# Operand placement, the first MLP quarter's order and the last output tiles of a two-layer hybrid decoder trunk

## The chip, the cores and the metric

The kernel runs on one core of one Trainium2 chip. The metric is the device time of one execution in microseconds; the median of several runs is compared. A profile of one execution gives, for each engine, every instruction with its start and duration. TensorE multiplies matrices (PE; its weight loads are shown as PEld), VectorE (DVE) and ScalarE (ACT) work elementwise, GpSimd (POOL) does so too and issues some DMAs, and SyncE (SP) issues the other DMAs.

## The reference

One sequence of 512 tokens, width 1024, passes two layers. Each has a token mixer, an MLP with a squared ReLU and a gated per-layer embedding; a norm ends the trunk.

```python
for i in range(DEPTH):                                   # DEPTH = 2
    hn = rmsnorm(h, norm_mix_g[i])
    h = h + (even_mixer(hn, ...) if i % 2 == 0 else odd_mixer(hn, ...))   # attention
    hn = rmsnorm(h, norm_mlp_g[i])
    u = jnp.square(jax.nn.relu(hn @ w_mlp_up[i]))        # 1024 -> 4096
    h = h + u @ w_mlp_down[i]                            # 4096 -> 1024
    gate = jax.nn.sigmoid(rmsnorm(h, norm_ple_g[i]) @ w_ple_gate[i])
    h = h + (p[i] @ w_ple_proj[i]) * gate
return rmsnorm(h, final_norm_g)
```

## The kernel before

All products run in a two-part format: an operand x is split into a high part hi (a rounded copy, made by ScalarE) and a low part lo = x - hi (a subtraction, by VectorE or GpSimd), and `mm3` (lines 145 to 149) issues three matmuls for one product: hi by hi, lo by hi, hi by lo. Activations are held transposed, features in the partitions and 512 tokens along the free dimension.

**The MLP of a layer** (`mlp`) goes in four quarters (`ch`) of the hidden width. A quarter has four up units (`up`, `c` = 0 to 3), each making 256 hidden columns, and then one down part (`down`). An up unit is either plain (two accumulators, 48 matmuls of 512 columns) or, for the pairs listed in `SEVEN`, computed as seven half-size products (Strassen's scheme, `up_products`, 84 matmuls of 256 columns). The seven-product units need sums and differences of the input's token halves: `combine_inputs(m)` makes them for two of the eight input tiles: two scaled copies by ScalarE (line 765), four differences on VectorE (753 to 756), a high part by ScalarE (769) and two low parts by GpSimd (771). All units of the first quarter (`ch` = 0) are plain, and the combinations are first used in the second quarter.

Each up unit ends in a chain over the single-buffered tile `u`: relu and scaling (844), square (845), differences (846 to 850), high part `uh` (852), low part `ul` (853), four buffers each.

**The down part** is also a seven-product scheme over halves of tokens and of output columns, and over two blocks `b` of hidden rows (`b` = 0 from units 0 and 1, `b` = 1 from units 2 and 3): `product(key, b, ...)`, 14 of them with 12 matmuls each. Their weights are loaded by `fetch` into two `raw` tiles and three `q` tiles (`quarter()`, three buffers, also used by the up units and by `combine_inputs(0)` and `(1)`); `put` adds one weight block onto another (912), `take` splits a block into high and low (779, 780); `collect` copies an accumulator out by ScalarE (929) and adds it into a DRAM array with a DMA. In the first quarter, before the change, combinations 2 and 3 are made within the down part, in the `u` buffer, and the products run 4, 1, 5 of block 0, then 1, 4 of block 1, 6 (0), 5 (1), 6 (1), 2 (0), 7 (0), 7 (1), 2 (1), 3 (0), 3 (1).

**The order of the work.** A planner puts each engine's instructions in an order at build time: an instruction is placed when, by a cost model, its inputs are ready and its engine is free, and among the ready ones the one written first goes first. `order(later, earlier)` adds an edge that the planner must respect. On the chip each engine runs its list strictly in that order, and so does SP its list of DMAs.

**Memory layout.** Pools lie one behind the other in the order of their opening, tiles within a pool in the order of first use of their tags, each rounded up to 32 bytes per partition: four built-in constants, cpool (ident, ones_r, eps_n, eps_s, h, gcols, gsub, neglam, lsum), wpool (raw, wh, wl), apool (hi, lo), spool (e, rs0, rcol, the small col tiles, rs1), and then, alternately, the mixer's pool and the MLP's pool `fpool`.

**The end of layer 1** (`ple_final`) makes the gated embedding and the final norm by tiles `t` of 128 tokens, columns 0 to 511 (`c` = 0) and then 512 to 1023 (`c` = 1). For `c` = 1 each tile has a sigmoid (1176), a product and a sum on VectorE (1177, 1178), a sum of squares (1184), for tiles 0 and 1 an inverse root by eleven operations on single columns (1193, 1194, 275 to 281), a scaling of the left half by ScalarE (1121) and of the right half by VectorE (1122), and output DMAs. The sigmoid's own accumulation runs 24 matmuls ahead of it; the last tile is cut in two pieces of 256 columns. Tiles 2 and 3 get their inverse roots together, by ScalarE's Ln and Exp and one Newton step, after the last piece; tile 3 is then sent as one DMA and tile 2 as two.

Of the kernel before, what the change touches and what calls it, by code (L numbers as in the profile page):

```python
# [12 lines left out]
F32 = mybir.dt.float32  # L13
# [6 lines left out]
P = 128  # L20
# [13 lines left out]
LOAD = (3, 1)  # L34
WARM = 10
# [29 lines left out]
def trunk(  # L65
# [29 lines left out]
    def col(name="c"):  # L95
        return spool.tile([P, 6], F32, tag="col", name=nm(name), bufs=10)
# [98 lines left out]

    ident = const([P, P], "ident")
# [5 lines left out]
    eps_n = const([P, 1], "eps_n")  # L202
    nc.vector.memset(eps_n, NORM_EPS)
    eps_s = const([P, 1], "eps_s")
# [81 lines left out]
    def tok_cols(rstd):  # L286
        rp = ps("tp")
        for t in range(QT):
            nc.tensor.transpose(rp[:, t * P:(t + 1) * P], rstd[:, t * P:(t + 1) * P], ident)
        rc = spool.tile([P, QT], F32, tag="rcol", name=nm("rcol"), bufs=2)  # L290
        nc.vector.tensor_scalar(rc, rp.rearrange("p (t c) -> p t c", c=P)[:, :, 0], -0.5, None, op0=ALU.mult)
        return rc
# [4 lines left out]
    gcols = const([P, 49], "gcols")  # L297
    gsub = const([P, 1], "gsub")
    neglam = const([P, 1], "neglam")
# [35 lines left out]
    def prepare():  # L335
# [19 lines left out]
        lsum = const([P, 2], "lsum")  # L355
# [36 lines left out]
    def mixer(layer, norm, nxt):  # L392
        st = ExitStack()
        mpool = st.enter_context(tc.tile_pool(name=f"mpool{layer}", bufs=2))
        mix[:] = [mpool]
# [12 lines left out]
        keep = [] if layer else [mpool.tile([P, S + 8], F32, tag=f"keep{x}", name=nm("keep"), bufs=1) for x in range(2)]  # L408
# [335 lines left out]
    def mlp(layer, fpool, norm, nxt):  # L744
# [13 lines left out]
        def combine_inputs(m):  # L758
            if m < 2:
                u = quarter().rearrange("p a c -> p (a c)").rearrange("p (a c) -> p a c", a=4)  # L760
            else:
                u = fpool.tile([P, 7, HW], F32, tag="u", name=nm("u"), bufs=1)[:, 0:4]
            for j in range(2):
                k = 2 * m + j
                nc.scalar.activation(
                    u[:, 2 * j:2 * j + 2].rearrange("p a c -> p (a c)"), h[k], AF.Copy, scale=gcol(1, layer, k))
            differences(u)
            hi, lo = (fpool.tile([P, 4, HW], F32R, tag=f"{t}{m}", name=nm(t), bufs=1) for t in ("th", "tl"))
            nc.scalar.activation(hi, u, AF.Copy)
            for x in (slice(0, 2), slice(2, 4)):  # L770
                nc.gpsimd.tensor_tensor(lo[:, x], u[:, x], hi[:, x].bitcast(F32), op=ALU.subtract)
            (h0, l0), (h1, l1) = ahl[2 * m], ahl[2 * m + 1]
            left, right = slice(0, HW), slice(HW, S)
            combos.append({T1: (hi[:, 0], lo[:, 0]), T3: (hi[:, 1], lo[:, 1]), T4: (hi[:, 2], lo[:, 2]), T2: (hi[:, 3], lo[:, 3]),
                           B11: (h0[:, left], l0[:, left]), B21: (h1[:, left], l1[:, left]), B22: (h1[:, right], l1[:, right])})
# [114 lines left out]
        def down(ch):  # L890
# [55 lines left out]
            take(0, A22, "5")  # L946
            take(1, A11, "1")
# [4 lines left out]
            put(0, A22, A11)  # L952
# [4 lines left out]
            take(1, A22, "5")  # L957
            product("4", 1, T4, "4")
# [3 lines left out]
            take(0, A12, "2")  # L962
            take(1, A22, "6")
            if first:
                combine_inputs(2)
# [16 lines left out]
            product("2", 0, B21, "1", "mm")  # L982
# [4 lines left out]
            if first:  # L987
                combine_inputs(3)
# [56 lines left out]
        for ch in range(NCH):  # L1045
            for c in range(4):
                up(ch, c)
                if (ch, c) in ((0, 1), (0, 2)):
                    combine_inputs(c - 1)
# [66 lines left out]
    def ple_final(layer, fpool, norm, pj, rest, quarter, hk, gb, ssqn):  # L1116
        ahl = norm.hl
        ssq = [fpool.tile([P, 3], F32, tag=f"ssq{t}", name=nm("ssq"), bufs=1) for t in range(QT)]

        def finish(t, r, left, right):  # L1120
            nc.scalar.activation(hk[t][:, 0:512], hk[t][:, 0:512], AF.Copy, scale=r)
# [18 lines left out]
        for c in range(2):  # L1140
# [27 lines left out]
            for t in range(QT):  # L1168
                last = c == 1 and t == QT - 1
                for i, (c0, n) in enumerate(parts[t]):  # L1170
# [5 lines left out]
                    sg = nc.scalar.activation(gt, accs[t][i][:, 0:n], AF.Sigmoid, scale=rc[:, t:t + 1])  # L1176
                    nc.vector.tensor_tensor(gt, gt, pj[4 * c + t][:, c0:c0 + n], op=ALU.mult)
# [10 lines left out]
                if t <= QT - 2:  # L1188
                    m, r, w = (fpool.tile([P, 2], F32, tag="fin", name=nm("fin"), bufs=6) for _ in range(3))
                x = slice(t // (QT - 1), t // (QT - 1) + 1)  # L1190
                sq = ssq[t]
                small = nc.gpsimd if last else nc.vector
                small.tensor_tensor(m[:, x], sq[:, 0:1], sq[:, 1:2], op=ALU.add)
                small.tensor_scalar(m[:, x], m[:, x], 1.0 / D, NORM_EPS, op0=ALU.mult, op1=ALU.add)
                if t < QT - 2:
                    rsqrt_cols(r[:, x], m[:, x], w[:, x])
                    finish(t, r[:, x], nc.sync, nc.sync)
                elif last:
                    tables = use_tables([sg.ins])
                    ln = nc.scalar.activation(r[:, 0:1], m[:, 0:1], AF.Ln)  # L1200
                    order(ln.ins, tables)
                    nc.scalar.activation(r[:, 1:2], sq[:, 2:3], AF.Ln, scale=1.0 / D, bias=m[:, 1:2])
                    nc.scalar.activation(r, r, AF.Exp, scale=-0.5)
                    nc.vector.scalar_tensor_tensor(m[:, 1:2], sq[:, 2:3], 1.0 / D, m[:, 1:2], op0=ALU.mult, op1=ALU.add)
                    newton(r, m, w)
        finish(QT - 1, r[:, 1:2], nc.sync, None)
        finish(QT - 2, r[:, 0:1], nc.scalar, nc.sync)

# [104 lines left out]
```

## Time and profile before

| | us |
|---|---|
| median of 3 runs | 1284.85 (1284.69 to 1286.22) |
| profiled execution, its own time | 1284.56 |
| span of its instructions | 1282.7 |
| TensorE busy in the span | 1258.7 |
| VectorE busy | 1074.7 |
| ScalarE busy | 786.9 |
| GpSimd busy | 273.2 |

The profile has a page and answers to queries. A row of a group of instructions reads: line, engine, operation, output<-inputs, shape, count | busy us, mean ns of one | idle time before them and what ended it. A row of a timeline reads: start us, duration, engine, line, operation, and in brackets the idle time of the engine before it and what released it. A row of a stretch reads: from:to, length, then busy us and count for each engine, the share of the clock that TensorE was granted, the DMA engines' busy share and GB/s. Matmuls are pipelined, so the duration of one (some 0.4 us) is longer than the distance from one start to the next; distances are a stretch's length over the number of starts.

### The profile page before, as it was taken

What the parts mean: (1) busy time and instruction counts of PE and PEld (TensorE: products, weight loads), DVE (VectorE), ACT (ScalarE), POOL (GpSimd) and SP (SyncE); (2) the same over time, 40 slices, a digit from 0 to 9 for tenths busy, and PEclk for the clock granted to TensorE, in tenths of its full rate; (3) what the DMA queues carried; (4) which work ended last, traced back from release to release, by engine and by line L of the source; (5) the groups of instructions that cost most, each with busy time, mean ns of one, the idle gap of its engine ahead of it and who ended that gap; (6) DMA issues with size and microseconds to landing.
All of it is one profiled execution on the core that took longest, in us unless ns stands there. A gap on an engine that the chain in (4) does not pass through costs nothing.

```text
span 1282.7 us, 18283 instructions
## 1 busy us (share of the span) xinstructions
PE 1258.7 (98%) x6802; PEld 1078.1 (84%) x6802; DVE 1074.7 (84%) x1685; ACT 786.9 (61%) x1291; POOL 273.2 (21%) x236
## 2 busy tenths in 40 slices
PE   9999999999899999999999999999999999999996
PEld 7988887888698898988889888788878889888885
DVE  7788898798888898889777777887898988988866
ACT  6667868575565565555556666765555656555563
POOL 3443433410210200200034333221112020020101
PEclk9999999999999999999999999999999999999998
DMA  6322414241372843944233212122426356286421
GB/s 223 135 84 82 142 64 140 81 147 52 118 199 55 200 136 99 249 143 134 99 132 102 87 67 88 61 91 82 132 79 168 115 119 193 60 226 223 129 69 66
DMA packets 44026, 156.25 MB, mean 122 GB/s; under 512 B 5089, under 2 KB 5825, under 8 KB 35361
## 3 DMA queue, kind: packets, MB, share of 16 engines
q1 hardware_dynamic: 35440, 139.62, 31.8%
q0 software_dynamic: 8064, 14.68, 7.6%
q8 instruction: 53, 0.87, 0.3%
q10 hardware_dynamic: 432, 0.79, 0.2%
q14 instruction: 37, 0.30, 0.1%
HBM read 129.82 MB, written 23.15 MB: 119 GB/s over the span
## 4 chain that ended last, share of the span: by engine, by line
PE 81%; DVE 10%; ACT 4%; issue 2%; POOL 1%; DMA 1%; SPq 0%; DVEq 0%; ACTq 0%
PE mm L145 11%; PE mm L148 11%; PE mm L149 11%; PE tp L145 5%; PE tp L149 5%; PE tp L148 5%; PE sc L145 5%; PE sc L149 5%; PE sc L148 5%; PE pv L145 4%; PE pv L149 4%; PE pv L148 4%; PE pv L585 2%; PE tp L564 2%; PE sc L541 1%
## 5 line engine op out<-in xcount | busy, mean ns | idle before, releaser
L130 POOL TENSOR_TENSOR wl<-raw,wh 128x512 fp32r<-128x512 f32 (+1 forms) x132 | 180.3, 1389 | 284.4 <-ACT wh L126 267.2
L145 PE MATMUL mm<-hi,wh 128*128 128x512 f32 (+1 forms) x456 | 175.6, 385 | 0.5 <-DVE tmp L502 0.4
L149 PE MATMUL mm<-hi,wl 128*128 128x512 f32 (+1 forms) x456 | 173.5, 381 | 0.0
L148 PE MATMUL mm<-lo,wh 128*128 128x512 f32 (+1 forms) x456 | 173.3, 380 | 0.0
L126 ACT ACTIVATE wh<-raw 128x1024 fp32r<-128x1024 f32 (+1 forms) x116 | 118.8, 1028 | 55.4 <-PE mm L148 22.4
L780 DVE TENSOR_TENSOR wl<-q,wh 128x1024 fp32r<-128x1024 f32 x88 | 107.5, 1222 | 30.2 <-ACT wh L779 30.1
L779 ACT ACTIVATE wh<-q 128x1024 fp32r<-128x1024 f32 x88 | 93.0, 1057 | 62.6 <-DVE q L912 19.9
L149 PEld LDWEIGHTS mm<-hi,wl 128*128 128x128 f32 x456 | 85.8, 188 | 16.9
L145 PEld LDWEIGHTS mm<-hi,wh 128*128 128x128 f32 x456 | 85.8, 188 | 15.4 <-DVE tmp L502 0.8
L148 PEld LDWEIGHTS mm<-lo,wh 128*128 128x128 f32 x456 | 85.9, 188 | 13.2
L780 DVE TENSOR_TENSOR wl<-raw,wh 128x1024 fp32r<-128x1024 f32 x72 | 88.9, 1235 | 3.9 <-ACT wh L779 3.9
L853 DVE TENSOR_TENSOR ul<-u,uh 128x1792 fp32r<-128x1792 f32 x32 | 64.8, 2024 | 32.4 <-ACT uh L852 32.4
L558 ACT ACTIVATE e<-e,cols 128x128 f32<-128x128 f32 (+3 forms) x96 | 53.8, 561 | 60.3 <-DVE cols L555 59.9
L779 ACT ACTIVATE wh<-raw 128x1024 fp32r<-128x1024 f32 x72 | 76.0, 1056 | 22.6 <-PE mm L149 6.6
L852 ACT ACTIVATE uh<-u 128x1792 fp32r<-128x1792 f32 x32 | 54.5, 1704 | 38.4 <-DVE u L850 38.4
L932 POOL DMA_DIRECT2D part<-e x24 | 25.9, 1138 | 228.0 <-ACT e L929 228.0
L132 DVE TENSOR_TENSOR wl<-raw,wh 128x1024 fp32r<-128x1024 f32 x50 | 62.8, 1262 | 9.8 <-ACT wh L126 9.8
L573 DVE TENSOR_TENSOR ptl<-tp,pth 128x128 fp32r<-128x128 f32 (+1 forms) x112 | 54.0, 485 | 6.4 <-ACT pth L572 6.1
L572 ACT ACTIVATE pth<-tp 128x128 fp32r<-128x128 f32 (+1 forms) x112 | 47.7, 429 | 18.9 <-PE tp L564 18.4
L145 PE MATMUL sc<-wh,uh 128*128 128x512 f32 x128 | 51.8, 405 | 4.5 <-ACT e L929 4.5
L145 PE MATMUL tp<-wh,uh 128*128 128x512 f32 x128 | 51.8, 405 | 2.8 <-DVE e L998 2.8
L149 PE MATMUL mm<-wh,lo 128*128 128x256 f32 x192 | 54.3, 283 | 0.0
(402 smaller groups left out, 3903.0 us busy)
## 6 DMA issues: line engine op xcount, KB each, us to landing
raw<-in_w_up_dram SPq DMA_DIRECT2D x32, 1024.0 KB, 6.4
raw<-in_w_in_dram SPq DMA_DIRECT2D x23, 1024.0 KB, 4.9
q<-in_w_down_dram SPq DMA_DIRECT2D x32, 512.0 KB, 4.1
raw<-in_w_down_dram SPq DMA_DIRECT2D x32, 512.0 KB, 4.6
part<-e POOLq DMA_DIRECT2D x48, 256.0 KB, 7.2
raw<-in_w_gate_dram SPq DMA_DIRECT2D x8, 1024.0 KB, 5.6
bias<-urow SPq DMA_DIRECT2D x24, 256.0 KB, 3.3
raw<-in_w_outa_dram SPq DMA_DIRECT2D x8, 768.0 KB, 4.2
```

The source lines that it names most:

```text
L126: act = nc.scalar.activation(hi, src, AF.Copy)
L130: nc.gpsimd.tensor_tensor(lo[:, kx], src[:, kx], hi[:, kx].bitcast(F32), op=ALU.subtract)
L132: last_low[:] = [nc.vector.tensor_tensor(lo, src, hi.bitcast(F32), op=ALU.subtract).ins]
L145: mm = nc.tensor.matmul(acc, lh, rh, start=start, stop=False, skip_group_check=again)
L148: nc.tensor.matmul(acc, lh, rl, start=False, stop=False, skip_group_check=again)
L149: return mm.ins, nc.tensor.matmul(acc, ll, rh, start=False, stop=stop, skip_group_check=again).ins
L558: nc.scalar.activation(e[:, 0:n], e[:, 0:n], AF.Exp, scale=-1.0, bias=mn, accum_out=s)
L573: evicts[:] = [a.ins, nc.vector.tensor_tensor(dl, src, dh.bitcast(F32), op=ALU.subtract).ins]
L779: high[:] = [nc.scalar.activation(hi, src, AF.Copy).ins]
L780: low[:] = [nc.vector.tensor_tensor(lo, src, hi.bitcast(F32), op=ALU.subtract).ins]
L852: nc.scalar.activation(uh, u, AF.Copy)
L853: part = nc.vector.tensor_tensor(ul, u, uh.bitcast(F32), op=ALU.subtract)
```

## The change

Four things are edited.

1. Small tiles move: in cpool all of them (gcols, eps_n, eps_s, gsub, neglam, lsum) stand first, and rcol, col and keep go to a pool `small` behind the mixer's pool.
2. `combine_inputs` uses a `q` tile for every combination and VectorE for the low part, in one instruction; in the first quarter combination 0 follows up unit 0, combination 1 unit 1, combinations 2 and 3 unit 2.
3. In the first quarter's down part product 2 of block 0, with the split of its weights, is moved ahead of block 1's products, and two weight additions are ordered behind the last up unit's last difference and behind the split of product 5's weights.
4. At the end, tile 2 gets its inverse root by column operations and is finished like tiles 0 and 1; a tile's scaling by ScalarE is ordered behind the next tile's sigmoid (up to tile 2's); the last tile alone is left for Ln, Exp and Newton, and is sent as two DMAs from two queues.

```diff
+COMBINE = ((0,), (1,), (2, 3), ())
...
     def col(name="c"):
-        return spool.tile([P, 6], F32, tag="col", name=nm(name), bufs=10)
+        return mix[1].tile([P, 6], F32, tag="col", name=nm(name), bufs=10)
...
+    gcols = const([P, 49], "gcols")
+    eps_n, eps_s, gsub, neglam = (const([P, 1], t) for t in ("eps_n", "eps_s", "gsub", "neglam"))
+    lsum = const([P, 2], "lsum")
     ident = const([P, P], "ident")
...
-        rc = spool.tile([P, QT], F32, tag="rcol", name=nm("rcol"), bufs=2)
+        rc = mix[1].tile([P, QT], F32, tag="rcol", name=nm("rcol"), bufs=2)
...
-        mix[:] = [mpool]
+        small = st.enter_context(tc.tile_pool(name=f"small{layer}", bufs=2))
+        mix[:] = [mpool, small]
...
-        keep = [] if layer else [mpool.tile([P, S + 8], F32, tag=f"keep{x}", ...
+        keep = [] if layer else [small.tile([P, S + 8], F32, tag=f"keep{x}", ...
...
         def combine_inputs(m):
-            if m < 2:
-                u = quarter().rearrange("p a c -> p (a c)").rearrange("p (a c) -> p a c", a=4)
-            else:
-                u = fpool.tile([P, 7, HW], F32, tag="u", name=nm("u"), bufs=1)[:, 0:4]
+            u = quarter().rearrange("p a c -> p (a c)").rearrange("p (a c) -> p a c", a=4)
...
-            for x in (slice(0, 2), slice(2, 4)):
-                nc.gpsimd.tensor_tensor(lo[:, x], u[:, x], hi[:, x].bitcast(F32), op=ALU.subtract)
+            nc.vector.tensor_tensor(lo, u, hi.bitcast(F32), op=ALU.subtract)
...
             take(0, A22, "5")
+            if first:
+                take(0, A12, "2")
             take(1, A11, "1")
             take(1, A22, "4")
             product("4", 0, T4, "4", "mm")
             product("1", 0, B11, "0", "tp")
             product("5", 0, T1, "2", "sc")
-            put(0, A22, A11)
+            if first:
+                product("2", 0, B21, "1", "mm")
+            s2a = put(0, A22, A11)
+            if first:
+                order(s2a, hidden[ch, 3][5])
...
             take(1, A22, "5")
+            if first:
+                after = low[0]
             product("4", 1, T4, "4")
...
-            take(0, A12, "2")
+            if not first:
+                take(0, A12, "2")
             take(1, A22, "6")
-            if first:
-                combine_inputs(2)
             product("6", 0, T2, "0")
...
-            product("2", 0, B21, "1", "mm")
+            if not first:
+                product("2", 0, B21, "1", "mm")
...
-            if first:
-                combine_inputs(3)
...
                 up(ch, c)
-                if (ch, c) in ((0, 1), (0, 2)):
-                    combine_inputs(c - 1)
+                if ch == 0:
+                    for m in COMBINE[c]:
+                        combine_inputs(m)
...
+        scaled = []
+
         def finish(t, r, left, right):
-            nc.scalar.activation(hk[t][:, 0:512], hk[t][:, 0:512], AF.Copy, scale=r)
+            scaled[:] = [nc.scalar.activation(hk[t][:, 0:512], hk[t][:, 0:512], AF.Copy, scale=r).ins]
...
                     sg = nc.scalar.activation(gt, accs[t][i][:, 0:n], AF.Sigmoid, scale=rc[:, t:t + 1])
+                    if scaled and t <= QT - 2:
+                        order(scaled.pop(), sg.ins)
...
-                if t < QT - 2:
-                    rsqrt_cols(r[:, x], m[:, x], w[:, x])
-                    finish(t, r[:, x], nc.sync, nc.sync)
-                elif last:
...
-        finish(QT - 1, r[:, 1:2], nc.sync, None)
-        finish(QT - 2, r[:, 0:1], nc.scalar, nc.sync)
+                if not last:
+                    rsqrt_cols(r, m, w)
+                    finish(t, r, nc.sync, nc.sync)
+        tables = use_tables([sg.ins])
+        ln = nc.scalar.activation(r, sq[:, 2:3], AF.Ln, scale=1.0 / D, bias=m)
+        order(ln.ins, tables)
+        nc.scalar.activation(r, r, AF.Exp, scale=-0.5)
+        nc.vector.scalar_tensor_tensor(m, sq[:, 2:3], 1.0 / D, m, op0=ALU.mult, op1=ALU.add)
+        newton(r, m, w)
+        finish(QT - 1, r, nc.scalar, nc.sync)
```

More of the change, by code (lines that the diff above doesn't have):

```diff
@@ L201, in trunk @@
     nc.vector.tensor_copy(ones_r, ones_d)
-    eps_n = const([P, 1], "eps_n")
     nc.vector.memset(eps_n, NORM_EPS)
-    eps_s = const([P, 1], "eps_s")
     nc.vector.memset(eps_s, SUBLN_EPS)
@@ L296, in trunk @@
     h = [hall[:, k] for k in range(KT)]
-    gcols = const([P, 49], "gcols")
-    gsub = const([P, 1], "gsub")
-    neglam = const([P, 1], "neglam")
     def gcol(kind, layer, k):
@@ L354, in prepare @@
         nc.vector.tensor_tensor(lamt[:, 0:2, :], lamt[:, 0:2, :], lamt[:, 2:4, :], op=ALU.mult)
-        lsum = const([P, 2], "lsum")
         nc.vector.reduce_sum(lsum, lamt[:, 0:2, :], axis=AX.X)
@@ L407, in mixer @@
         pt_i = [0]
-        keep = [] if layer else [mpool.tile([P, S + 8], F32, tag=f"keep{x}", name=nm("keep"), bufs=1) for x in range(2)]
+        keep = [] if layer else [small.tile([P, S + 8], F32, tag=f"keep{x}", name=nm("keep"), bufs=1) for x in range(2)]
         keep_i = [0]
@@ L1187, in ple_final @@
                     continue
-                if t <= QT - 2:
-                    m, r, w = (fpool.tile([P, 2], F32, tag="fin", name=nm("fin"), bufs=6) for _ in range(3))
-                x = slice(t // (QT - 1), t // (QT - 1) + 1)
+                m, r, w = (fpool.tile([P, 1], F32, tag="fin", name=nm("fin"), bufs=6) for _ in range(3))
                 sq = ssq[t]
                 small = nc.gpsimd if last else nc.vector
-                small.tensor_tensor(m[:, x], sq[:, 0:1], sq[:, 1:2], op=ALU.add)
-                small.tensor_scalar(m[:, x], m[:, x], 1.0 / D, NORM_EPS, op0=ALU.mult, op1=ALU.add)
-                if t < QT - 2:
-                    rsqrt_cols(r[:, x], m[:, x], w[:, x])
-                    finish(t, r[:, x], nc.sync, nc.sync)
-                elif last:
[L1199 to L1205, printed above, removed]
-        finish(QT - 1, r[:, 1:2], nc.sync, None)
-        finish(QT - 2, r[:, 0:1], nc.scalar, nc.sync)
+                small.tensor_tensor(m, sq[:, 0:1], sq[:, 1:2], op=ALU.add)
+                small.tensor_scalar(m, m, 1.0 / D, NORM_EPS, op0=ALU.mult, op1=ALU.add)
+                if not last:
[8 more added lines that the diff above has]
+        finish(QT - 1, r, nc.scalar, nc.sync)
     sig_tail, ahead = [], [blk0]
```

## The prediction

> **What bounds the kernel now.** I read the page's busy shares first, then stretches of the MLP against each other, then the engines' timelines where two stretches differ, and the tail last.
>
> ```profile
> PE 1258.7 (98%) x6802; PEld 1078.1 (84%) x6802; DVE 1074.7 (84%) x1685; ACT 786.9 (61%) x1291; POOL 273.2 (21%) x236
> ```
>
> TensorE is busy nearly always. Time can come out of the spacing of its matmuls, out of its pauses, or out of the end, where it has finished. The stretches show all three (length, then busy time and count for PE, PEld, DVE, ACT, POOL, then clock, DMA share, GB/s):
>
> ```profile
> core 0: us, PE busy (x) PEld busy (x) DVE busy (x) ACT busy (x) POOL busy (x), PEclk, DMA share, GB/s
> 280.48:313.17 32.69, 32.69 (x145) 27.05 (x144) 27.66 (x30) 17.46 (x19) 5.99 (x4) 1.00 0.34 111
> 313.17:357.97 44.80, 41.24 (x169) 32.49 (x168) 39.11 (x44) 26.72 (x33) 11.52 (x6) 0.96 0.36 112
> 399.29:438.45 39.16, 39.16 (x170) 31.57 (x169) 34.95 (x37) 21.86 (x26) 7.04 (x8) 1.00 0.45 100
> ...
> 933.31:978.46 45.15, 41.42 (x170) 32.59 (x168) 42.91 (x46) 26.61 (x33) 10.06 (x6) 0.96 0.39 116
> ```
>
> The first row is three up units of layer 0's first quarter: 3 x 48 = 144 matmuls of 512 columns start in it (x also counts one still running), 32.69/144 = 0.2270 us each. The others are the 14 products of 12 matmuls in one quarter's down part, 168 starts. The second quarter needs 39.16 us without a pause, 0.2331 each. The first quarters of the two layers need 44.80 and 45.15, so 5.64 and 5.99 us more for the same matmuls, at a mean clock of 0.96.
>
> *Spacing.* What differs between 0.2270 and 0.2331 is where operands lie. Tiles are laid one behind the other and rounded up to 32 bytes; the 12 small tiles of spool (rcol, col) put 384 bytes in front of every later pool. So uh, ul, th, tl, q, pth, v, kh start 384 (448 behind keep) past a multiple of 512, while wh, wl, hi, lo lie on multiples. Up units read only the latter; the down products have uh, ul as stationary operand. In the last projection's second half uh, ul are the moving operand against aligned hi, lo (three tiles of 24 matmuls; PE columns alone):
>
> ```profile
> 1249.51:1266.30 16.79, 16.79 (x73) 1.00 0.08 31
> ```
>
> 16.79/72 = 0.2332, with hardly a DMA beside it: either operand off its multiple shows the same 6 ns. For 256 columns there is no such loss (48 starts each; first with th, tl moving, then aligned):
>
> ```profile
> 359.40:365.10 5.70, 5.70 (x51) 5.70 (x49) 3.45 (x5) 1.99 (x5) 0.72 (x1) 1.00 1.04 266
> 670.02:675.78 5.76, 5.76 (x50) 5.76 (x49) 4.20 (x6) 3.58 (x5) 2.89 (x2) 1.00 0.05 20
> ```
>
> 0.1188 against 0.1200: aligned is 1.2 ns slower, if anything. VectorE's mean times (1222 and 1235 ns, q off, raw on a multiple) show no penalty either:
>
> ```profile
> L780 DVE TENSOR_TENSOR wl<-q,wh 128x1024 fp32r<-128x1024 f32 x88 | 107.5, 1222 | 30.2 <-ACT wh L779 30.1
> ...
> L780 DVE TENSOR_TENSOR wl<-raw,wh 128x1024 fp32r<-128x1024 f32 x72 | 88.9, 1235 | 3.9 <-ACT wh L779 3.9
> ```
>
> *Pauses.* In layer 0's first quarter, timelines of ScalarE, GpSimd, TensorE, then the clock of the stretch:
>
> ```profile
> 331.59 1.06 ACT L769 ACTIVATE th<-u 128x1024 fp32r<-128x1024 f32 x1 [1.88 <-DVE u L756]
> 332.73 1.06 ACT L779 ACTIVATE wh<-raw 128x1024 fp32r<-128x1024 f32 x1
> 338.48 0.72 ACT L765 ACTIVATE u<-h,gcols 128x512 f32<-128x512 f32 x1 [4.69 <-POOL tl L771]
> ...
> 340.67 1.06 ACT L929 ACTIVATE e<-sc 128x512 f32<-128x512 f32 x2
> ```
> ```profile
> 332.73 5.71 POOL L771 TENSOR_TENSOR tl<-u,th 128x512 fp32r<-128x512 f32 x2 [43.84 <-ACT th L769]
> ```
> ```profile
> 341.29 0.79 PE L145 MATMUL sc<-wh,uh 128*128 128x512 f32 x1 [2.85 <-ACT e L929]
> ```
> ```profile
> 338.05:344.43 6.38, 3.53 (x10) 0.73 0.22 83
> ```
>
> Combination 2 leaves its low part to GpSimd (5.71 us for two halves). Combination 3 writes the same single u buffer, so its first ScalarE copy (L765) stands 4.69 us in ScalarE's queue, and behind it the evictions L929 that product 7 needs on its bank. TensorE pauses 2.85 us and then runs cold (0.73 over the stretch). Layer 1 has the same wait and a later one on the bank of product 3, whose VectorE reader is late:
>
> ```profile
> PE tp L145 <- DVE e L998: 2.1, 2, 1.8
> PE sc L145 <- ACT e L929: 1.6, 1, 1.6
> ```
>
> **The change part by part.**
>
> *Alignment.* Moving small tiles to the front of cpool (with the four built-in constants they fill exactly 512 bytes) and to a pool of their own behind the mixer's puts every large tile on a multiple of 512. Each down part loses 39.16 - 168 x 0.2270 = 1.02 us, eight of them 8.2; the last projection 72 x 0.0062 = 0.45. Attention has some 120 misaligned matmuls of 512 columns; they don't run in a clean stretch, so between 0 and 0.7, I take 0.4. The seven-product units have 16 x 84 = 1344 matmuls of 256 columns, 5 in 7 of them with a moved operand: 960 x 1.2 ns = 1.2 us lost, or nothing. Net -7.9; ends -9.3 and, if the place is not the cause, 0.
>
> The Trainium skill, page SBUF — State Buffer, section "Door 1: The DMA port swizzle", speaks against this part: an access pays for each new 16-byte line that it crosses into. All tiles start on multiples of 32 bytes before and after, so by that rule this part gives 0 and the sum below would be 1273.8 instead of 1265.9. The trace so far does not agree, by the 0.2332 above.
>
> *Combinations on VectorE, and the new order of the first quarter.* What VectorE gains and what covers it:
>
> ```profile
> L853 DVE TENSOR_TENSOR ul<-u,uh 128x1792 fp32r<-128x1792 f32 x3 | 6.1, 2023 | 3.7 <-ACT uh L852 3.7
> ...
> L756 DVE SCALAR_TENSOR_TENSOR q<-q 128x256 f32<-128x256 f32 x1 | 0.4, 420 | 0.0
> ```
> ```profile
> 320.18 2.03 DVE L853 TENSOR_TENSOR ul<-u,uh 128x1792 fp32r<-128x1792 f32 x1 [0.69 <-ACT uh L852]
> ```
> ```profile
> 285.96 3.28 SPq L899 DMA_DIRECT2D q<-in_w_down_dram  x2
> 296.51 0.80 SPq L899 DMA_DIRECT2D raw<-in_w_down_dram  x2
> ```
> ```profile
> raw<-in_w_down_dram SPq DMA_DIRECT2D x32, 512.0 KB, 4.6
> ```
>
> Both GpSimd waits go: at most 11.6 us (5.64 + 5.99), cold clock included. VectorE gets four subtractions of 1.22 = 4.9, and the eight differences of combinations 2 and 3 (0.42 each, 3.4) move from the down part into the up units: 8.3 us per layer into a stretch where it idles 32.69 - 27.66 = 5.0 (3.7 of it waiting for uh). So 3.3 spill over. The unit they would delay is the last: its ul ends at 322.2 and is needed half-way through the first product of block 1, after three products of 2.80 (12 x 0.2331) and a half, at 323.0. With product 2 moved ahead of block 1 that becomes 325.8, a margin of 3.6: just cover; I charge 0.5 a layer. ScalarE gets two combinations more (2 x 0.72 + 1.06 each, 5.0 us) against 15 idle: nothing. Product 7 now follows product 6 directly on one bank, so L929 (0.53 a copy) is no longer hidden under product 2: between 0.1 and 1.6 (a split copy of 1.06 ahead in the queue), I take 0.5 a layer. The split of A12 is wanted 14 us sooner, with its product at 321.6, so by 319.3; its load, second of the two at 296.51, landed near 301.5. SP takes it behind three loads into q buffers that now wait for a combination each: 17 us of room, nothing charged. Total -11.6 + 2 x 1.0 = -9.6; ends -11.6 and 0.
>
> *The last output tiles.* ScalarE, VectorE, transfers:
>
> ```profile
> 1268.20 0.72 ACT L1121 ACTIVATE nat<-nat,fin 128x512 f32<-128x512 f32 x1 [2.60 <-DVE fin L277]
> 1268.83 0.67 ACT L1176 ACTIVATE q<-pv,rc 128x512 f32<-128x512 f32 x1
> ...
> 1277.60 0.38 ACTq L1127 DMA_DIRECT2D out_dram<-nat  x1
> ```
> ```profile
> 1274.64 0.08 DVE L1181 DVE_READ_ACCUMULATOR2_ANT ssq<- 128x1 f32 x1
> ...
> 1276.24 1.42 DVE L1122 SCALAR_TENSOR_TENSOR nat<-nat,fin,gb 128x512 f32<-128x512 f32 x2
> ```
> ```profile
> L275 DVE TENSOR_TENSOR fin<-fin 128x1 f32<-128x1 f32 x6 | 1.0, 160 | 0.2
> ```
> ```profile
> out_dram<-nat SPq DMA_DIRECT2D x1, 512.0 KB, 2.6
> out_dram<-nat ACTq DMA_DIRECT2D x1, 256.0 KB, 3.2
> ```
>
> Now two tiles are scaled at the end (1.42) and the last transfer lands at 1277.60 + 3.2 = 1280.8. After, one tile of 512 KB is left: scaled by 1277.0, landed 2.6 later at 1279.6, so -1.2. Tile 2's sigmoid no longer stands behind tile 1's scaling (2.60 us of waiting), up to 2.3 us sooner; but tile 2's nine column operations more (0.16 each) and its scaling (0.71) now run on VectorE among tile 3's halves, 2.2 us in front of the 1274.64. I let these cancel; ends -0.6 and +0.9. Part -1.2, ends -2.2 and +0.5.
>
> Sum against the profiled execution's own 1284.56: -7.9 - 9.6 - 1.2 = -18.7, 1265.9 us. The median of the runs shown, 1284.85, is 0.3 higher, a difference I leave out.
>
> **The rivals.**
>
> *Place is not the cause* (the spacing belongs to the products themselves): the first part gives 0; 1284.56 - 9.6 - 1.2 = 1273.8. For it: nothing but scatter of aligned matmuls elsewhere; against: the last projection's row. The Trainium skill's page cited above gives this time.
>
> *VectorE becomes the bound of the first quarter.* If the 8.3 us find none of the idle time, the last unit comes 8.3 - 3.6 = 4.7 us late and TensorE runs cold afterwards (0.73 over 6 us, some 1.2 us): 5.9 a layer, as much as now. 1284.56 - 7.9 - 1.2 = 1275.5. For it: DVE 39.11 of 44.80 busy already; against: its idle time lies between the units' steps, where short operations fit.
>
> *Weights late in SP's queue, slower than before.* If the third combination holds its q buffer long, the three q loads stand and A12 behind them. Each us after 319.3 is a us of pause per layer. The rest gives 20.7, so it turns slower once A12 lands after 319.3 + 10.3 = 329.6, issued after 325. At 328 issue: 1284.56 - 20.7 + 2 x 13.3 = 1290.5. Against: 28 us later than now.
>
> *The change doesn't do what it says*: neither the first part nor the second acts, and the tail alone is left, 1283.4.
>
> **How the numbers follow.** Forecast 0.70, place not the cause 0.12, VectorE 0.10, SP 0.04, neither 0.04. The likeliest is 1265.9, its own range 1260.5 to 1271 (ends of the parts that don't lie in a rival). Reaching over the first two rivals gives 1260.5 to 1275.5, leaving out about 0.1 to 0.2. About 0.2% is what a measurement of this kernel can tell from no change. Faster: the forecast, the first two rivals and 0.01 of the last, 0.93; same 0.02; slower the SP rival and 0.01, 0.05.
>
> **What would show it.** Alignment: second-quarter down parts of 38.1 instead of 39.16 us, the 72 matmuls at 0.227; units of 256 columns unchanged or 0.1 us longer. First quarter: 39 to 40 us in both layers, clock 1.00, no GpSimd subtraction, short waits on L929's successor. Tail: one 512 KB tile behind the last column operations. Wrong would be: down spacing still 0.233; a TensorE wait for ul or wl at the start of block 1; SP issues of down weights after 320.

## The result, and the profile after

The changed kernel takes 1271.07 us (median of four runs, 1270.20 to 1272.38) against 1285.37 (1284.69 to 1286.22, now four runs of the kernel before as well): a ratio of 0.989, 95% interval 0.9875 to 0.9904. So 14.3 us are gone where 18.7 were forecast. The profiled execution took 1271.77, with a span of 1270.0. It is read here by the views that the prediction used.

Busy share on the page of the kernel after:

```profile
PE 1251.0 (99%) x6802; PEld 1075.1 (85%) x6802; DVE 1071.5 (84%) x1704; ACT 787.5 (62%) x1290; POOL 243.2 (19%) x220
```

TensorE's busy time fell by 7.7 us for the same 6802 matmuls and the span by 12.7; the other 5.0 us are pauses and the end. Stretches of the kernel after (length, then busy time and count of PE, PEld, DVE, ACT, POOL, clock, DMA share, GB/s): the first quarter of layer 0, the second quarter of layer 0, the first quarter of layer 1, the three units behind the second quarter; then, PE alone, the 72 matmuls of the last projection.

```profile
315.01:354.06 39.05, 38.89 (x169) 31.20 (x168) 36.69 (x37) 23.90 (x28) 1.92 (x2) 1.00 0.40 130
395.50:434.00 38.50, 38.50 (x169) 31.31 (x168) 34.48 (x35) 21.86 (x26) 7.05 (x8) 1.00 0.44 100
927.48:967.26 39.78, 39.15 (x169) 31.14 (x168) 36.67 (x37) 23.95 (x28) 1.75 (x2) 1.00 0.40 126
434.00:475.54 41.54, 41.54 (x301) 39.38 (x300) 37.20 (x54) 25.03 (x35) 1.73 (x2) 1.00 0.60 174
```
```profile
1237.49:1253.81 16.32, 16.32 (x74) 1.00 0.08 32
```

The first quarters went from 44.80 and 45.15 to 39.05 and 39.78, at a clock of 1.00 and with GpSimd left almost idle. The second quarter went from 39.16 to 38.50, not to the 38.1 of the forecast. The last projection hit its number: 16.32/72 = 0.2267 us a matmul.

Why 38.50 and not 38.14 (168 x 0.2270): ScalarE, then TensorE, in the second quarter of the kernel after.

```profile
413.92 1.06 ACT L774 ACTIVATE wh<-q 128x1024 fp32r<-128x1024 f32 x1 [2.67 <-DVE q L907]
```
```profile
414.66 0.39 PE L146 MATMUL mm<-wh,uh 128*128 128x512 f32 x1
415.04 0.50 PE L146 MATMUL tp<-wh,uh 128*128 128x512 f32 x1
415.37 0.40 PE L146 MATMUL pv<-wh,uh 128*128 128x512 f32 x1
```

From start to start these are 0.38 and 0.33 us instead of 0.227: 0.25 us lost. The product starts 0.06 us behind the end of ScalarE's copy (413.92 + 1.06 = 414.98), and that copy waited for VectorE's sum. TensorE has become quick enough to meet VectorE's chain of sums and splits. In the kernel before the same copy ends 0.09 us ahead of its product (417.94 + 1.06 = 419.00), and the place costs 0.08 (0.31 from start to start instead of 0.233). ScalarE, then TensorE, in the kernel before:

```profile
417.94 1.06 ACT L779 ACTIVATE wh<-q 128x1024 fp32r<-128x1024 f32 x1 [2.67 <-DVE q L912]
```
```profile
419.09 0.47 PE L145 MATMUL tp<-wh,uh 128*128 128x512 f32 x1
419.40 0.39 PE L145 MATMUL pv<-wh,uh 128*128 128x512 f32 x1
```

One more start of that quarter comes 0.06 us late in the kernel after. Without these places, worked out from the starts in the traces, the matmuls stand 0.2326 us apart in the kernel before and 0.2273 in the kernel after.

In the first quarter of layer 0 VectorE has hardly a gap left (VectorE, then TensorE):

```profile
326.51 2.03 DVE L848 TENSOR_TENSOR ul<-u,uh 128x1792 fp32r<-128x1792 f32 x1 [0.69 <-ACT uh L847]
328.45 1.22 DVE L775 TENSOR_TENSOR wl<-raw,wh 128x1024 fp32r<-128x1024 f32 x1
329.59 1.22 DVE L907 TENSOR_TENSOR q<-q,q 128x1024 f32<-128x1024 f32 x1
330.73 1.22 DVE L907 TENSOR_TENSOR raw<-raw,raw 128x1024 f32<-128x1024 f32 x1
```
```profile
328.16 0.39 PE L146 MATMUL mm<-wh,uh 128*128 128x512 f32 x1
328.59 0.50 PE L150 MATMUL sc<-wh,ul 128*128 128x512 f32 x1
```

The last unit's ul ends at 328.54 and TensorE takes it at 328.59, 0.21 us late: the margin of 3.6 us that the prediction gave it is used up. All short pauses together are 39.05 - 38.14 = 0.9 us in layer 0 and 1.6 in layer 1, where one wait, for a bank that VectorE reads, is long enough to be listed (waits of TensorE in that stretch):

```profile
PE tp L146 <- DVE e L999: 0.5, 1, 0.5
```

The end of the run, ScalarE, then VectorE, then TensorE's last start:

```profile
1261.59 0.72 ACT L1125 ACTIVATE nat<-nat,fin 128x512 f32<-128x512 f32 x1 [3.02 <-DVE fin L279]
1262.21 0.46 ACT L1180 ACTIVATE q<-tp,rc 128x256 f32<-128x256 f32 x1
```
```profile
1263.97 0.08 DVE L1187 DVE_READ_ACCUMULATOR2_ANT ssq<- 128x1 f32 x1
```
```profile
1259.44 0.28 PE L150 MATMUL tp<-uh,lo 128*128 128x256 f32 x1
```

The last sigmoid (L1180) stands in ScalarE's queue behind tile 2's scaling, which waits 3.02 us for VectorE's column operations. It starts 2.8 us behind the last matmul, and the last sum of squares comes 4.5 us behind it (2.8 before, where the last matmul starts at 1271.88 and the sum comes at 1274.64). From there to the end are 6.0 us instead of 8.1. The two nearly cancel: 10.56 us from the last matmul's start to the end of the span, 10.85 before.

The first profiles also differ in a place that the change does not touch, ScalarE's wait for the first weights, first in the kernel after, then in the kernel before.

```profile
11.17 1.15 ACT L328 ACTIVATE wh<-raw 128x512 fp32r<-128x512 f32 x2 [2.32 <-DMA raw<-in_w_in_dram]
```
```profile
9.84 1.16 ACT L329 ACTIVATE wh<-raw 128x512 fp32r<-128x512 f32 x2 [0.83 <-DMA raw<-in_w_in_dram]
```

### The profile page after: what moved, and what is told of

Its sections match the earlier page's. It is cut to its first block, busy times and chain, and to the rows that moved or that the text cites. A ratio compares the mean times of both kernels' runs of the same rounds, so it can differ in the third digit from the quotient of the medians.

```text
span 1270.0 us, 18273 instructions
## 1 busy us (share of the span) xinstructions
PE 1251.0 (99%) x6802; PEld 1075.1 (85%) x6802; DVE 1071.5 (84%) x1704; ACT 787.5 (62%) x1290; POOL 243.2 (19%) x220
## 4 chain that ended last, share of the span: by engine, by line
PE 77%; DVE 11%; ACT 5%; issue 4%; DMA 2%; SPq 0%; POOL 0%; ACTq 0%; DVEq 0%; POOLq 0%
PE mm L146 10%; PE mm L149 10%; PE mm L150 10%; PE sc L150 5%; PE sc L149 5%; PE sc L146 5%; PE tp L146 5%; PE tp L149 4%; PE tp L150 4%; PE pv L146 4%; PE pv L149 4%; PE pv L150 4%; PE pv L584 2%; PE tp L563 2%; DVE qq L508 1%
## 5 line engine op out<-in xcount | busy, mean ns | idle before, releaser
L775 DVE TENSOR_TENSOR wl<-raw,wh 128x1024 fp32r<-128x1024 f32 x72 | 87.8, 1219 | 4.8 <-ACT wh L774 4.7
L133 DVE TENSOR_TENSOR wl<-raw,wh 128x1024 fp32r<-128x1024 f32 x50 | 60.8, 1219 | 9.7 <-ACT wh L127 9.7
L149 PE MATMUL mm<-wl,hi 128*128 128x256 f32 x192 | 54.2, 282 | 0.0
L146 PE MATMUL mm<-wh,hi 128*128 128x256 f32 x192 | 54.2, 282 | 0.0
```

The lines of the kernel that those rows point to most:

```text
L133: last_low[:] = [nc.vector.tensor_tensor(lo, src, hi.bitcast(F32), op=ALU.subtract).ins]
L146: mm = nc.tensor.matmul(acc, lh, rh, start=start, stop=False, skip_group_check=again)
L149: nc.tensor.matmul(acc, lh, rl, start=False, stop=False, skip_group_check=again)
L775: low[:] = [nc.vector.tensor_tensor(lo, src, hi.bitcast(F32), op=ALU.subtract).ins]
```

## The experiments

Each kernel was compared with the kernel before on the same chip. The table has the median time (of e5, e9 and e10 there is one run each) and, from one profile of each kernel, lengths of stages from its trace, in us, from the start of one matmul to that of another: the first projection; the first quarters' down parts (Q1) of both layers; the second quarter's (Q2) and the three units behind it, layer 0; the second half of the last projection (Last); from the last matmul to the end of the span (End).

| kernel | time | first proj. | Q1, layer 0 | Q1, layer 1 | Q2 | units | Last | End |
|---|---|---|---|---|---|---|---|---|
| before | 1285.37 | 24.43 | 44.80 | 45.15 | 39.15 | 41.32 | 22.37 | 10.85 |
| after | 1271.07 | 25.70 | 39.05 | 39.78 | 38.50 | 41.54 | 21.95 | 10.56 |
| e1 place alone | 1281.12 | 25.32 | 44.77 | 43.59 | 38.49 | 41.43 | 21.95 | 11.12 |
| e2 MLP tiles off | 1273.90 | 24.30 | 39.44 | 39.40 | 39.22 | 41.32 | 22.37 | 10.20 |
| e3 end as before | 1269.83 | 24.47 | 39.13 | 39.21 | 38.56 | 41.51 | 21.95 | 10.37 |
| e4 end, scalings last | 1271.48 | 25.31 | 40.12 | 39.31 | 38.54 | 41.45 | 21.95 | 11.17 |
| e5 places in steps | 1273.36 | 24.60 | 39.33 | 39.51 | 39.13 | 41.42 | 22.26 | 10.27 |
| e6 product 2 back | 1271.92 | 25.78 | 39.93 | 40.43 | 38.54 | 41.43 | 21.95 | 10.54 |
| e7 low parts on GpSimd | 1288.82 | 25.75 | 45.14 | 45.49 | 38.49 | 41.43 | 21.95 | 11.00 |
| e8 end, tile 2 back | 1270.43 | 25.53 | 39.04 | 39.03 | 38.49 | 41.77 | 21.95 | 9.41 |
| e9 uh, ul 384 off | 1276.61 | 25.63 | 39.43 | 40.58 | 39.14 | 41.44 | 22.37 | 10.16 |
| e10 uh, ul 256 off | 1272.39 | 25.55 | 38.97 | 39.40 | 38.56 | 41.44 | 21.95 | 10.54 |
| e11 best | 1269.12 | 25.05 | 39.21 | 39.59 | 38.52 | 41.32 | 21.95 | 9.54 |
| e12 after again | 1270.98 | 24.99 | 39.11 | 39.41 | 38.57 | 41.43 | 21.95 | 10.55 |

**Place: e1, e2.** e1 is the kernel before with the hunks on `gcols`, `eps_n` and the other constants, `col`, `rcol` and `keep`. e2 is the kernel after with one line:

```
     def mlp(layer, fpool, norm, nxt):
+        fpool.tile([P, 96], F32, tag="pad", name=nm("pad"), bufs=1)
```

> The kernel before with the small tiles moved as in the change and nothing else: the order of instructions on every engine is that of before. Theory (the spacing of 512-column matmuls follows the place of their operands): the quarters 2 and 3 of the down parts start to end in 38.1 to 38.5 us instead of 39.15, the last projection's 72 matmuls at 0.227, the units of 256 columns 0.1 to 0.3 us longer each, the first quarters' pauses unchanged: 4 to 8 us less than before, 1277.5 to 1281.5. Rival (place is not the cause, the new order or shorter VectorE queues are): 39.15 and 0.2332 as before, 1285.4.

> The kernel after with one unused tile of 384 bytes at the head of the MLP's pool, so that uh, ul, u, q, th, tl stand 384 bytes past a multiple of 512 again; same instructions in the same order on every engine. Theory (place): the quarters 2 and 3 go back to 39.15 us, the last projection to 0.2332, the units of 256 columns to 29.40; 4 to 7 us slower than after, 1275 to 1278. Rival (place is not the cause): as after, 1271.1.

e1 took 1281.12 (1279.93 to 1282.51) against 1285.84, ratio 0.9964 (0.9951 to 0.9978). e2 took 1273.90 (1273.28 to 1274.75), ratio 0.9909 (0.9895 to 0.9923). The second quarter in e1, and in e2 the second quarter and the three units behind it:

```profile
400.19:438.68 38.49, 38.49 (x169) 31.28 (x168) 34.44 (x35) 21.85 (x26) 7.04 (x8) 1.00 0.45 101
```
```profile
393.74:432.96 39.22, 39.22 (x169) 31.51 (x168) 34.99 (x37) 21.85 (x26) 7.04 (x8) 1.00 0.44 102
```
```profile
432.96:474.28 41.32, 41.32 (x302) 39.12 (x300) 36.72 (x53) 25.05 (x35) 1.73 (x2) 1.00 0.59 172
```

With the same instructions in the same order, 384 bytes switch the quarter between 38.5 and 39.2 us. Place is a cause by itself, worth 4.7 us in e1. e1 has the 38.49 too, so what is missing to 38.14 does not come from the other parts of the change. Its first quarter of layer 0 keeps its pauses (44.77); that of layer 1 is 1.6 shorter, which stays unexplained. e2 is only 2.9 us slower than the kernel after (e12 below), less than the theory's 4. In the profiles its second to fourth quarters and last projection are 4.9 us longer than those of e12; its units (1.2 shorter, in part by the place), its start (0.7) and its end (0.35) give some of that back.

**Which tile, and which multiple: e5, e9, e10.** e5 puts the four buffers at different places; e9 and e10 move only uh and ul (96 and 32 elements, or 64 and 64):

```
+            return [fpool.tile([P, 7 * HW + n], F32R, ...)[:, 0:7 * HW]... for t, n in (("uh", 32), ("ul", 8))]
...
+        fpool.tile([P, 96], F32, tag="padh", ...)        # e10: 64
             uh, ul = ...
+            padded.append(fpool.tile([P, 32], F32, tag="padu", ...))   # e10: 64
```

> The kernel after with 128 bytes behind each uh buffer, 32 behind each ul buffer and 384 behind them all, so that the four uh buffers (units 0 to 3 of a quarter) start 0, 128, 256 and 384 bytes past a multiple of 512, the four ul buffers 0, 32, 64 and 96, and everything behind them on multiples again (u at 128); same instructions in the same order. Read from the spacing of the down products by buffer. If only multiples of 512 are quick: unit 0 at 0.2270, units 1, 2, 3 alike near 0.2325. If 256 (or 128, 64) is enough: those units at 0.2270 too. If place is not the cause: all four alike.

> The kernel after with 384 unused bytes in front of uh and ul and 128 behind them, so that only uh and ul (the stationary operands of the down products) stand 384 bytes past a multiple of 512; u, q, th and tl lie as in after; same instructions in the same order. If the place of uh and ul sets the spacing: quarters 2 and 3 in 39.15 us, the last projection at 0.233, the units of 256 columns at 41.43 as in after. If another tile's place does (u, which VectorE and ScalarE write and read beside the products): 38.5 us and 0.2267.

> As the run with uh and ul 384 bytes off, with 256 instead, everything else on multiples of 512. If a multiple of 256 is enough: quarters 2 and 3 in 38.5 us as in after, the last projection at 0.2267. If only multiples of 512 are quick: 39.15 us and 0.233.

e5 could not be read by buffer. Worked out from the starts in its trace (gaps over 0.28 us left out), all four units run at 0.231 to 0.234 us a matmul, where the kernel after has 0.227 to 0.228: unit 0, whose uh and ul lie on multiples of 512, is as slow as the others (0.232). A product alternates between two units every six matmuls, and one that is off seems to slow its neighbours too. The start of the second quarter in e5 shows it: matmuls 1, 6, 7, 8 and 13.

```profile
394.04 0.39 PE L146 MATMUL sc<-wh,uh 128*128 128x512 f32 x1
...
395.17 0.40 PE L150 MATMUL tp<-wh,ul 128*128 128x512 f32 x1
395.40 0.40 PE L146 MATMUL sc<-wh,uh 128*128 128x512 f32 x1
395.64 0.39 PE L149 MATMUL sc<-wl,uh 128*128 128x512 f32 x1
...
396.81 0.40 PE L146 MATMUL tp<-wh,uh 128*128 128x512 f32 x1
```

The first six are unit 0's and run at 0.226 (1.13 us from the first to the sixth). With the seventh, unit 1's first (uh 128 past a multiple, ul 32 past), the spacing goes to 0.235 (1.41 us for six), and it stays there when unit 0 comes again. Moving all buffers alike gives the answer. The second quarter and the 72 matmuls of the last projection, in e9, then in e10:

```profile
395.34:434.48 39.14, 39.14 (x169) 31.54 (x168) 34.87 (x35) 21.86 (x26) 7.04 (x8) 1.00 0.44 99
```
```profile
1242.26:1259.05 16.79, 16.79 (x73) 1.00 0.08 31
```
```profile
394.37:432.93 38.56, 38.56 (x170) 31.32 (x169) 34.47 (x35) 21.84 (x26) 7.04 (x8) 1.00 0.43 100
```
```profile
1238.12:1254.44 16.32, 16.32 (x74) 1.00 0.08 32
```

uh and ul alone are the cause: with only them 384 off, 39.14 and 16.79/72 = 0.2332. And 512 is more than is needed: 256 off costs nothing (38.56, 0.2267). 128 was not tried by itself: in e5 it is slow, but there ul is 32 off beside it. Nor was uh moved without ul. The Trainium skill, page SBUF — State Buffer, section "Door 1: The DMA port swizzle", counts lines of 16 bytes that an access crosses into; 256 and 384 are both multiples of that, so its rule makes no difference between e9 and e10, and the runs show one of 6.5 ns a matmul.

**The combinations: e6, e7.** e6 puts product 2 and its split back; e7 gives the low parts to GpSimd and keeps all else:

```
-            if first:
-                product("2", 0, B21, "1", "mm")
             s2a = put(0, A22, A11)
...
-            if not first:
-                product("2", 0, B21, "1", "mm")
+            product("2", 0, B21, "1", "mm")
```
```
-            nc.vector.tensor_tensor(lo, u, hi.bitcast(F32), op=ALU.subtract)
+            for x in (slice(0, 2), slice(2, 4)):
+                nc.gpsimd.tensor_tensor(lo[:, x], u[:, x], hi[:, x].bitcast(F32), op=ALU.subtract)
```

> The kernel after with product 2 of the first quarters back between products 6 and 7, its split back too; the combinations stay on VectorE among the up units. If the new order is needed (it gives VectorE's late ul of the last unit 2.7 us more): TensorE waits 1.3 to 2.7 us for that ul at the start of block 1, the first quarters take 40.5 to 42 us instead of 39.1 to 39.8: 1273.5 to 1276. If the combinations on VectorE did it all: 39 to 40 us and 1271.1, or up to 1 us less, since product 7 no longer waits for the eviction of its bank.

> The kernel after with the low parts of all four combinations on GpSimd again (two halves each), the combinations still among the up units, product 2 where after has it. If it was the place of combinations 2 and 3 (inside the down part, on one shared buffer) that cost, not the engine, and VectorE's queue is what holds the first quarters now: first quarters of 38.2 to 38.8 us, 1270. If the engine was the cause: the q buffers are held some 4.5 us longer, the down weights come late behind them, first quarters over 40 us, 1273 or more.

e6: first quarters of 39.93 and 40.43, 0.8 and 1.0 longer than in e12 (39.11 and 39.41). At the start of block 1, the place that the new order was made for, the starts in the traces show 0.9 us lost in both layers of e6 and 0.3 in the kernel after. So the order is worth some 0.6 us a quarter, less than its theory expected and more than its rival. The rest is not clear of scatter: a later wait for a bank comes and goes with the order unchanged (e4 has 40.12 in layer 0). The time itself, 1271.92 (1270.69 to 1275.15), cannot tell it from the kernel after.

e7 sank the theory that the place of the combinations was the fault: 1288.82 (1284.15 to 1292.87), ratio to the kernel before 1.0023 (1.0009 to 1.0037). All of the second part's gain is gone, though no combination stands inside the down part. The first quarter of layer 0 and TensorE's waits in it; then VectorE's first two differences of combinations in one stretch of the up units in e7, the GpSimd operations there, two other VectorE operations there, and one of the same differences in the kernel after:

```profile
314.45:359.59 45.14, 40.98 (x170) 32.27 (x168) 39.35 (x42) 26.05 (x31) 1.92 (x2) 0.96 0.34 109
```
```profile
PE pv L146 <- DVE u L840: 1.9, 1, 1.9
PE tp L146 <- DVE e L1000: 1.3, 2, 0.9
PE sc L150 <- DVE ul L849: 1.0, 1, 1.0
```
```profile
L753 DVE TENSOR_TENSOR q<-q 128x256 f32<-128x256 f32 x1 | 1.5, 1507 | 0.0
L752 DVE TENSOR_TENSOR q<-q 128x256 f32<-128x256 f32 x1 | 0.7, 749 | 2.6 <-ACT q L761 2.6
```
```profile
L767 POOL TENSOR_TENSOR tl<-q,th 128x512 fp32r<-128x512 f32 x6 | 8.4, 1435 | 3.7 <-ACT th L765 3.7
```
```profile
290.43 1.79 DVE L216 SCALAR_TENSOR_TENSOR rs<-e,rs 128x512 f32<-128x512 f32 x1
```
```profile
300.03 2.88 DVE L849 TENSOR_TENSOR ul<-u,uh 128x1792 fp32r<-128x1792 f32 x1 [1.98 <-ACT uh L848]
```
```profile
L753 DVE TENSOR_TENSOR q<-q 128x256 f32<-128x256 f32 x1 | 0.4, 415 | 0.0
```

Subtractions of 0.42 us take 0.75 and 1.51 beside GpSimd's. That agrees with the Trainium skill, page SBUF — State Buffer, section "Who interferes with whom": a VectorE instruction with two inputs in SBUF contends with a GpSimd instruction that reads SBUF. The other two take 1.79 and 2.88 where they take 0.69 and 2.02 in the kernel after. So VectorE is spared three low parts of 1.22 us in that stretch, 3.7, and loses 3.4 by these four delays. The last units come late, and TensorE loses most of its time within the down part, by the waits for VectorE shown (4.2 us) and a clock of 0.96. The engine was the cause. It was not by late weights, as had been expected with it: no wait of TensorE, ScalarE or VectorE from 286 to 331 us names a transfer. How the whole 18 us divide between VectorE's delay and GpSimd's own slowness was not separated.

**The end: e3, e4, e8.** e3 has the end of the kernel before; e4 orders tile 2's scaling behind the last sigmoid and takes its second half off VectorE; e8 is e3 with the order of the scalings of after.

```
 e4:-                    if scaled and t <= QT - 2:
    +                    if scaled and (t <= QT - 2 or i == 1):
    ...
    +                    nc.gpsimd.tensor_tensor(hk[t][:, 512:1024], hk[t][:, 512:1024], gb[:, 512:1024], op=ALU.mult)
 e8, on the end of before:
    +            scaled[:] = [nc.scalar.activation(hk[t][:, 0:512], hk[t][:, 0:512], AF.Copy, scale=r).ins]
    ...
    +                    if scaled and t <= QT - 2:
    +                        order(scaled.pop(), sg.ins)
```

> The kernel after with the last output tiles finished as in the kernel before (two tiles scaled together at the end). By the prediction's step the tail is worth 1.2 us: 1272.3, and 11.5 us from TensorE's last matmul to the end of the span. By the reading of the trace after (the last sigmoid now stands 2.5 us behind tile 2's scaling, which gives back what the shorter end saves) it is worth 0.3: 1271.4, with the last sigmoid 0.1 us behind the last matmul.

> The kernel after with tile 2's scaling behind the last sigmoid on ScalarE, and its second half scaled by ScalarE too (multiplied by gb on GpSimd first) so that VectorE has 0.75 us less among tile 3's halves. If the queue in front of the last sigmoid is what kept the tail from its gain: the last sum of squares comes 0.42 + 0.75 = 1.2 us sooner and the end with it, 1269.9, below both kernels. If VectorE's column operations of tile 2 or the last transfers hold the end anyway: 1271.1, no change.

> The kernel after with the last two tiles finished together as in the kernel before, but tile 1's scaling still behind tile 2's sigmoid. If the new place of the scalings is the good half of the tail's change and taking tile 2 out of the common end the bad one: the last sigmoid 0.4 us behind the last matmul, the last sum of squares at 2.3 instead of 4.6, the end 9.4 to 9.9 us behind the last matmul instead of 10.56, 0.7 to 1.1 us faster than after: 1270.2. If not: 10.4 to 10.6, 1271.1.

With the end of before, the span ends 10.85, 10.37 (e3) and 11.12 us (e1) behind the last matmul; with the end of after, 10.16 to 11.00 in eight profiles, 10.56 and 10.55 of them in the kernel after. The third part of the change is worth nothing that can be told. The median of e3, 1269.83 (1268.81 to 1271.48), is even 1.2 us below the kernel after's, where both readings expected it above; the ranges overlap. e4 failed (11.17). Its sigmoid came at 0.4 us, but the load of ScalarE's tables for the last logarithm had slipped behind the two scalings, and GpSimd's product slowed VectorE again (ScalarE, then GpSimd and VectorE in e4):

```profile
1261.74 0.71 ACT L1127 ACTIVATE nat<-nat,fin 128x512 f32<-128x512 f32 x1
1262.46 1.28 ACT L221 ACT_TABLE_LOAD   x1
```
```profile
1257.26 1.30 POOL L1200 TENSOR_TENSOR nat<-nat,gb 128x512 f32<-128x512 f32 x1 [12.87 <-ACT q L1194]
```
```profile
1257.86 0.97 DVE L1187 TENSOR_TENSOR q<-q,pj 128x256 f32<-128x256 f32 x1
```
```profile
1260.93 0.42 DVE L1187 TENSOR_TENSOR q<-q,pj 128x256 f32<-128x256 f32 x1
```

The last half's product (1260.93) also stood behind tile 2's column operations in VectorE's queue, 1.7 us after the sigmoid that it reads had ended at 1259.26. So the rival that e4 was given, that these operations hold the end anyway, is part of the answer.

e8 ended at 9.41, inside what was expected (1270.43, 1268.68 to 1275.04). In e8, ScalarE, then VectorE:

```profile
1258.85 0.47 ACT L1180 ACTIVATE q<-tp,rc 128x256 f32<-128x256 f32 x1 [1.26 <-PE tp L150]
```
```profile
1260.65 0.08 DVE L1187 DVE_READ_ACCUMULATOR2_ANT ssq<- 128x1 f32 x1
```

The last matmul starts at 1258.47, so the sigmoid stands 0.4 us behind it and the sum of squares 2.2, half of the 4.5 in the kernel after. By these profiles the good half of the third part is the order of the scalings (e3 to e8, 10.37 to 9.41); taking tile 2 out of the common end is the bad half, by its column operations and the scaling in front of the last sigmoid.

**A better version and the control: e11, e12.** e11 is e8 with 384 bytes between ul and u (`padu` of 96 elements, none in front).

> The kernel after with the end of the run that put tile 2 back (9.41 us behind the last matmul), and with 384 unused bytes behind ul, so that uh and ul keep their multiples of 512 and u, q, th, tl stand 384 past one. If the 256-column matmuls gain from that as before: the units between the down parts take 41.31 us instead of 41.43, the down parts stay at 38.5: 1.1 us from the end and 0.7 from the units, 1269.3 and below the control. If their 1.2 ns has another cause: 41.43 and 1270.

> The kernel after once more, unchanged, as the control of this call and for the scatter of its start. If the 1.3 us that the start lost in the first profile are scatter of the first transfers: the first projection anywhere from 24.3 to 25.8 us, the attention of layer 0 near 234.6, a median of 1270.5 to 1271.5. If the change did it: 25.7 again.

e11 took 1269.12 (1268.63 to 1269.63), ratio 0.9876 (0.9859 to 0.9892); e12, beside it, 1270.98 (1270.29 to 1272.53), ratio 0.9891 (0.9876 to 0.9906). The intervals of the ratios overlap, the runs do not: 1.9 us. The three units behind the second quarter, e11, then e12:

```profile
432.81:474.13 41.32, 41.32 (x301) 39.13 (x300) 37.12 (x54) 25.05 (x35) 1.73 (x2) 1.00 0.60 174
```
```profile
432.72:474.15 41.43, 41.43 (x301) 39.33 (x300) 37.21 (x54) 25.02 (x35) 1.72 (x2) 1.00 0.60 174
```

The matmuls of 256 columns do run a little faster off the multiple, 0.11 us in three units. And the start of e12 took 24.99 us where the first profile had 25.70. Over all 14 profiles it lies between 24.30 and 25.78, whatever the kernel, and it follows ScalarE's copy that waits for the first weights: the copy starts at 9.71 us in e2, which has the 24.30, and at 11.28 in e6, which has the 25.78. It is scatter of the first transfers.

## Why the prediction was right, and where it was not

The direction, the wide range (1260.5 to 1275.5) and the mechanisms of the first two parts held; the third part's did not, and the forecast of 1265.9 was 5.2 us below the median. By its own steps:

- *Alignment, -7.9.* The mechanism is shown: e2, e9 and e10 change only places, and the spacing follows them to 0.2267 and 0.2332 in the last projection, as worked out. The term "each down part loses 39.16 - 168 x 0.2270 = 1.02 us, eight of them 8.2" is the step that failed. Quarters 2 and 3 became 0.65 shorter, quarter 4 0.88 (40.79 to 39.91), and the first quarters 0.0 to 0.3 (e2 against e12). The step took TensorE's spacing for the whole of a stage and did not ask what came next. In the second quarter the spacing itself gave 0.9 (0.2326 to 0.2273), and short waits took 0.24 of that back: 0.31 us in the kernel after, 0.08 in the kernel before, where the 39.16 already held them. The longest stands behind VectorE's chain of sums and splits. That is read from the trace; no run took the wait away. Whole, e1 measures -4.7. The last projection was right (-0.42 for 0.45). Attention, at 0.4, was too high: layer 0's takes 234.5 us in the kernel before and 234.6 to 234.7 in most profiles with the new places, layer 1's is not separated. The loss in the 256-column units was half of the 1.2 us charged: 0.11 for three of 16 units.
- *Combinations and order, -9.6.* With places held off (e2) the first quarters fall from 44.80 and 45.15 to 39.44 and 39.40: -11.1, better than -9.6. The charges for VectorE and the eviction were right in kind (the last ul arrives as TensorE needs it), yet while TensorE runs at 0.233 they hardly show. They show once it runs at 0.227: 39.05 and 39.78, or 0.9 and 1.6 above 38.14. Some 0.7 of the 1.6 is the wait for a bank, which is not there in e8 (39.03). The wait for ul at the start of block 1, one of the signs of being wrong, came true at 0.2 us. So the two first parts are not additive. For the first quarters the sum had 9.6 + 2.0 = 11.6 us, and the kernel after has 11.1; that these are close is luck, for the second part alone gave 11.1 and place next to nothing.
- *The last tiles, -1.2.* Wrong in the step "I let these cancel". Tile 2's column operations don't only share VectorE with tile 3: tile 2's scaling waits for them on ScalarE, in front of the last sigmoid. That costs 1.8 us up to the last sum of squares and gives back what the shorter end saves (2.1). They are also eleven more, not nine: two for the first guess of the root, then nine. e8 removes that wait and gets 1.1.
- *The start, nothing.* Right, but the profile of before that the sum started from had one of the quickest starts (24.43 in a scatter of 24.30 to 25.78), which is part of the distance.
- *The range.* The favourable ends of the parts, -9.3, -11.6 and -2.2, give 1261.5; the lower end of 1260.5 is 1.0 too low. The result, 1271.07, lies at the very end of the forecast's own range (1271).
- *The rivals.* "Place is not the cause" is excluded by e2 and e9. "VectorE becomes the bound of the first quarter" came true in small, 0.9 to 1.6 us a layer instead of 5.9. Late weights did not show: no TensorE wait of the first quarters names a transfer. "Doesn't do what it says" holds for the third part alone.

The profiled execution is 5.9 us above the forecast. By stages, the eight down parts gave 15.5 us instead of 8.2 + 9.6, which leaves 2.3 missing. The first projection took 1.3 more and the attention of layer 0 took 0.7 more instead of up to 0.4 less; both scatter from profile to profile (that attention took 235.25 us, 234.5 in the kernel before, 234.6 to 234.7 in most others and 237.9 in e6). The end gave 0.3 instead of 1.2. The rest, some 0.5, lies in the units and what follows them. The median of the four runs lies 0.7 lower.

## What to carry to other kernels

When a stage of one engine is shortened by a few per cent, look for the operand that now arrives within that margin; the gain ends there. Before an operation is moved off a path, see which queue it lands in and what stands behind it: one scaling in front of the last sigmoid took back the whole of an otherwise sound edit. And try places with a pad: it changes no instruction, and the spacing of the matmuls shows the effect at once.

## What was not expected of the hardware

- For these 512-column matmuls, uh and ul 256 bytes past a multiple of 512 are as good as on it (0.2267 us), and 384 past are not (0.2332). With buffers at mixed places the spacing goes up at the first one that is off (e5, 0.226 to 0.235), and well-placed ones behind it run slow too. Why is open.
- GpSimd's low parts, put among VectorE's operations to spare it work, cost VectorE nearly as much as they spared: subtractions of 0.42 us became 0.75, 0.97 and 1.51.
- The first projection of identical work takes 24.30 to 25.78 us from run to run by its first transfers, more than the third part of this change could be worth.
